# A decoder layer on one core: prompt attention's value product by key-value group, on high and low parts

## The chip, the core and the metric

The kernel runs on one core of a Trainium2 chip. The core has a matrix engine (PE, its weight loads listed as PEld), a vector engine (DVE), a scalar engine (ACT), GpSimd (POOL) and a sync engine (SP) that issues most DMAs. Each engine takes its instructions strictly in the order in which the program lists them; semaphores tie the engines together. SBUF holds the working tiles, PSUM has eight banks of 128x512 fp32 into which PE writes. The metric is the time of one execution on the device in microseconds (us), the median of several runs.

## What is computed

One decoder layer for a prompt of 1024 tokens and for 8 sequences with 4 new tokens each (the sample). Cut to the part around the change, for one chunk of 128 prompt tokens:

```python
def nsa_attend(q, ..., gates):            # 8 query heads, 2 key-value groups, 4 heads per group, head size 64
    p_c = masked_softmax(q . k_cmp);  o_c = p_c @ v_cmp      # compressed blocks: 63 keys
    p_s = masked_softmax(q . k_sel);  o_s = p_s @ v_sel      # selected blocks (all earlier keys for this length)
    p_w = masked_softmax(q . kv_win); o_w = p_w @ v_win      # window of 512 keys
    return g0 * o_c + g1 * o_s + g2 * o_w
```

Beside attention the layer has a state-space part (a scan over 128 steps, a kernel K, a product Y), a GLU on it, an output projection (the mix) and a feed-forward net (FFN). Everything is fp32; sums must keep nearly fp32 accuracy.

## The kernel before, in words

In the order of the span: projections and compression (0 to about 440 us), prompt attention with what is put between its units (about 457 to 950 us), the mix (to about 1085 us), the FFN (to the end).

**Prompt attention** (`phase_attend`) takes the eight chunks of 128 queries in the order 4, 0, 6, 1, 7, 2, 5, 3. Chunk c has, for branch 0 (selected), c+1 key tiles of 128 keys, for branch 1 (window), at most 5, and the compressed branch with 64 keys. A *unit* is a chunk, a branch and four heads. In before, unit `hf` holds heads 2hf, 2hf+1, 4+2hf, 5+2hf, two of each key-value group. `attend_scores` makes a unit's scores and exponentials: fp32r products into a two-bank tile (PSUM tag s), a reduction on DVE (`asm`), an exponential on ACT (`ap`). `attend_values` makes the unit's value product. The scores of the next unit are listed ahead of a unit's values.

**The value product** is made by `pv_tile`, once for each key tile of a unit: PE transposes the four heads' 128x128 probabilities into one PSUM bank (tag t, two banks), ACT or DVE in turn copies the bank to SBUF as fp32 (`pT`), and PE multiplies in plain fp32: two matmuls, one per group, of 64 value columns against 256 query columns, into 64 partitions each of the result bank `O` (tag o, one bank for both units of a branch). This is called a *turn* below. `attend_out` then copies O (128x512) on ACT, PE transposes it, DVE multiplies with the gate over the softmax sum, POOL adds to `att`. The compressed branch does the same with two turns of 64 keys.

**Between the units** stand pieces of other work, by the table PLAN: the sample's second half (A), the state-space kernel (K: products `Kp`, evicted on DVE and ACT to `K`, an addition `dd`, and eight DMAs on SP that spread `K` into `ssm_W`), the outputs Y (from `ssm_W` and the scan's state `ssm_H`), GLU (`gl`), adaLN columns (`ada`), the loading of the output weights (P). They use one PSUM bank of their own (tag f). The list scheduler that builds the program sets the final order on each engine.

**The scan** is 128 steps on DVE, four small SBUF-to-SBUF operations each (lines L1536 to L1539), spread between the other DVE work of chunks 4 and 0.

**The sample's second half** reads its caches through eight buffers `s_raw`; window rows come by SP's DMAs, selected rows by POOL's gathers, two runs of four ahead.

**The mix** (`mix_product`) makes three fp32r matmuls per weight tile from high and low parts of x and of the weights. Its first two row tiles (8 and 7) are listed in the midst of chunks 2, 5 and 3.

Of the kernel before, what the change touches and what calls it, by code (L numbers as in the profile page):

```python
# [89 lines left out]
class Kernel:  # L90
# [235 lines left out]
    def phase_sample(self):  # L326
# [22 lines left out]
        self.sample_begin(sb)  # L349
# [8 lines left out]
        self.compress_end(cp)  # L358
        self.second = self.sample_attend(1, sb)
# [5 lines left out]
        self.XT = "ff"  # L365
# [168 lines left out]
    def c_out(self, b, s, hid):  # L534
# [15 lines left out]
        else:  # L550
            for g in range(2):
                nc.tensor.matmul(p[:64, 64 * g:64 * g + 64], hid[:, g, :64], w2, start=True, stop=True)
            nc.vector.memset(self.vcp, 0.0)
            nc.vector.tensor_scalar(self.vcp[:64], p[:64, :128], 0.5, None, op0=ALU.mult)
# [107 lines left out]
    def sample_attend(self, half, sb):  # L662
# [6 lines left out]
        if half == 0:  # L669
            self.before = sb.tile([128, 30, 30], F32, name="before")  # L670
            o = CONST_AT["before"][0]
            nc.sync.dma_start(self.before.rearrange("p j i -> p (j i)"), A["consts"][:, o:o + 900])
# [51 lines left out]
        runs = [r for r in self.runs if r[0] == half]  # L724
# [7 lines left out]
        for k, run in enumerate(runs):  # L732
# [25 lines left out]
            self.sample_load(sb)  # L758
# [21 lines left out]
    def sample_begin(self, sb):  # L780

        self.runs = [(half, br, j) for half in range(2) for br, j in ((2, 0), (1, 0), (1, 1), (1, 2), (1, 3))]
        self.todo = list(self.runs)
        for _ in range(2):
            self.sample_load(sb)

    def sample_load(self, sb):
        if not self.todo:
            return
        half, br, j = run = self.todo.pop(0)  # L790
        raws = []
        for b in range(4 * half, 4 * half + 4):
            raw = sb.tile([128, 4, 256], F32, tag="s_raw", name=f"s_raw{br}{b}_{j}", bufs=8)
# [4 lines left out]
            raws.append(raw)  # L798
        self.raws[run] = raws
# [207 lines left out]
    def phase_attend(self):  # L1007
# [5 lines left out]
        self.psum("psc", s=2, t=2, o=1, f=1)  # L1013
# [5 lines left out]
        for n, c in enumerate(self.ORDER):  # L1019
# [8 lines left out]
            for br in range(2):  # L1028
                for hf in range(2):
                    ahead.append((c, br, hf, st, self.attend_scores(c, br, hf, st, pa)))  # L1030
# [12 lines left out]
    def between(self, c):  # L1043
# [4 lines left out]
        def part(i):  # L1048
            tags, self.tags = self.tags, "ff"
# [86 lines left out]
    def attend_setup(self, pc, pa):  # L1136
# [6 lines left out]
        self.mk = mk  # L1143
# [81 lines left out]
    def attend_values(self, c, br, hf, st, Ps, pc):  # L1225
# [3 lines left out]
        if hf == 0:  # L1229
            st["O"] = self.ps("o", f"aso{c}{br}")  # L1230
# [675 lines left out]
```

## Time and profile before

| | us |
|---|---|
| median of 3 runs (lowest, highest) | 1826.65 (1823.66, 1833.36) |
| the profiled execution, its own time | 1828.84 |
| its span in the profile | 1827.1 |
| PE busy | 1709.1 (94%) |
| DVE / ACT / POOL busy | 972.2 / 618.9 / 427.1 |
| mean granted PE clock of the execution | 0.979 |

The page gives busy time over the whole span; the share of a stage is read from the table by stretches. "Idle before" a row names what released it. A row with x4 covers four instructions; from the start of one row to the start of the next is what they cost on a busy engine, since the shown length of a matmul holds its pipeline too.

### The profile page before, as it was taken

How to read it: one execution, taken by the hardware profiler on the slowest of the kernel's cores; microseconds unless marked ns; L12 is line 12 of the kernel's file. 1: busy time of each engine (PE TensorE's matmuls, PEld its weight loads, DVE VectorE, ACT ScalarE, POOL GpSimd, SP SyncE). 2: the span in 40 equal slices, each digit the busy share in tenths (PEclk: the TensorE clock that was granted, in tenths of full speed). 3: DMA queues.
4: the chain of work that ended last, by engine and by line, in shares of the span. 5: the costliest groups of instructions: out<-in, count | busy, mean ns of one | idle time of the engine just before them, and what ended most of it. 6: DMA issues, size and time to landing. Idle time of an engine off the chain costs nothing.

```text
span 1827.1 us, 29355 instructions
## 1 busy us (share of the span) xinstructions
PE 1709.1 (94%) x11546; PEld 1439.4 (79%) x11546; DVE 972.2 (53%) x2330; ACT 618.9 (34%) x1247; POOL 427.1 (23%) x817
## 2 busy tenths in 40 slices
PE   6998999899796899999989989999999999999997
PEld 3898988788564665655657888998998999999996
DVE  4867647588988466566535443323333333333346
ACT  4523146455453355565433341111111111211210
POOL 2344545232015313341122210110110110110150
PEclk9999999899898999999999999999999999999999
DMA  8333243645231345413114221101201201201113
GB/s 297 105 86 106 70 152 119 219 157 193 65 112 63 71 161 195 152 61 104 55 60 138 92 93 58 58 24 50 67 24 47 70 24 47 70 24 47 53 47 141
DMA packets 132699, 172.43 MB, mean 94 GB/s; under 512 B 17176, under 2 KB 92312, under 8 KB 132304
## 3 DMA queue, kind: packets, MB, share of 16 engines
q1 hardware_dynamic: 123024, 136.62, 23.4%
q0 software_dynamic: 9408, 33.89, 5.8%
q8 instruction: 91, 1.49, 0.3%
q14 instruction: 48, 0.39, 0.1%
q10 hardware_dynamic: 128, 0.04, 0.0%
HBM read 143.88 MB, written 25.46 MB: 93 GB/s over the span
## 4 chain that ended last, share of the span: by engine, by line
PE 61%; DVE 6%; DMA 4%; ACT 2%; issue 1%; POOL 1%; SPq 1%; DVEq 0%; ACTq 0%; POOLq 0%
PE gu L1810 19%; PE dn L1853 13%; PE g L1810 5%; PE u L1810 4%; PE aso L1283 3%; PE as L1205 1%; PE as L1206 1%; SPq L1596 1%; PE acs L1258 1%; PE mx8M L1728 1%; PE mx2M L1728 1%; PE mx5M L1728 1%; PE mx0M L1728 1%; PE mx1M L1728 1%; PE mx4M L1728 1%
## 5 line engine op out<-in xcount | busy, mean ns | idle before, releaser
L1810 PE MATMUL gu<-h2h,wh 128*128 128x352 f32 x704 | 227.8, 324 | 5.0 <-ACT h2h L870 5.0
L1810 PE MATMUL gu<-h2h,wl 128*128 128x352 f32 x704 | 227.3, 323 | 0.0
L1810 PE MATMUL gu<-h2l,wh 128*128 128x352 f32 x704 | 226.8, 322 | 0.0
L1859 DVE TENSOR_TENSOR acc<-acc,dn 128x512 f32<-128x512 f32 x144 | 98.9, 687 | 229.9 <-PE dn L1853 229.9
L1818 POOL TENSOR_TENSOR al<-fa,ah 128x352 fp32r<-128x352 f32 (+1 forms) x66 | 69.6, 1054 | 414.8 <-ACT ah L1817 408.8
L1813 ACT ACTIVATE fa<-gu 128x352 f32<-128x352 f32 x44 | 20.4, 465 | 412.1 <-PE gu L1810 412.1
L1853 PE MATMUL dn<-dh,ah 128*128 128x512 f32 x352 | 140.3, 399 | 5.6 <-DVE fin L1862 5.2
L1810 PEld LDWEIGHTS gu<-h2h,wh 128*128 128x128 f32 x704 | 132.5, 188 | 7.9 <-ACT h2h L870 5.3
L1853 PE MATMUL dn<-dl,ah 128*128 128x512 f32 x352 | 138.7, 394 | 0.0
L1853 PE MATMUL dn<-dh,al 128*128 128x512 f32 x352 | 138.3, 393 | 0.0
L1810 PEld LDWEIGHTS gu<-h2l,wh 128*128 128x128 f32 x704 | 133.0, 189 | 3.8
L1810 PEld LDWEIGHTS gu<-h2h,wl 128*128 128x128 f32 x704 | 132.7, 188 | 3.1
L1816 DVE TENSOR_TENSOR fa<-fa,gu 128x352 f32<-128x352 f32 x44 | 22.9, 521 | 143.0 <-ACT fa L1813 143.0
L409 ACT CAST wh<-wr 128x1024 fp32r<-128x1024 f32 x44 | 46.0, 1048 | 151.8 <-PE g L1810 77.0
L1205 PE MATMUL as<-kst,aqA 128*128 128x320 f32 (+4 forms) x192 | 76.7, 403 | 16.2 <-ACT ap L1222 9.3
L1853 PEld LDWEIGHTS dn<-dh,ah 128*128 128x128 f32 x352 | 66.1, 188 | 24.5 <-ACT wh L409 7.5
L410 DVE TENSOR_TENSOR wl<-wr,wh 128x1024 fp32r<-128x1024 f32 x44 | 58.8, 1339 | 49.3 <-ACT wh L409 49.3
L1853 PEld LDWEIGHTS dn<-dl,ah 128*128 128x128 f32 x352 | 66.1, 188 | 15.6
L1853 PEld LDWEIGHTS dn<-dh,al 128*128 128x128 f32 x352 | 66.3, 188 | 8.1
L1222 ACT ACTIVATE ap<-as,asm 128x640 f32<-128x640 f32 (+3 forms) x64 | 55.8, 873 | 46.6 <-DVE asm L1221 31.3
L1221 DVE TENSOR_REDUCE asm<-as 128x1 f32<-128x640 f32 (+3 forms) x64 | 58.5, 918 | 20.7 <-PE as L1209 19.8
L1206 PE MATMUL as<-kst,aqB 128*128 128x320 f32 (+4 forms) x192 | 65.1, 344 | 4.7 <-ACT aqB L1168 4.7
(2137 smaller groups left out, 4667.9 us busy)
## 6 DMA issues: line engine op xcount, KB each, us to landing
wada<-in_w_ada SPq DMA_DIRECT2D x24, 1024.0 KB
wr<-in_w_ffn_gate SPq DMA_DIRECT2D x22, 512.0 KB
wr<-in_w_ffn_up SPq DMA_DIRECT2D x22, 512.0 KB
wd<-in_w_ffn_down SPq DMA_DIRECT2D x22, 512.0 KB
bx<-in_x_prompt SPq DMA_DIRECT2D x8, 512.0 KB
s_raw<-in_cache_kv_win SPq DMA_DIRECT2D x8, 512.0 KB
wor<-in_w_out SPq DMA_DIRECT2D x16, 256.0 KB
ex<-x_d SPq DMA_DIRECT2D x8, 512.0 KB
```

The lines of the kernel that those rows point to most:

```text
L409: self.nc.scalar.copy(hi, raw)
L410: self.nc.vector.tensor_tensor(lo, raw, hi.bitcast(F32), op=ALU.subtract)
L1205: nc.tensor.matmul(Sv, qA[:, h, :], kk, start=True, stop=False)
L1206: nc.tensor.matmul(Sv, qB[:, h, :], kk, start=False, stop=not mt)
L1221: nc.vector.tensor_reduce(mx[:, :1], Sv, axis=ax, op=ALU.max, negate=True)
L1222: nc.scalar.activation(Pv, Sv, AF.Exp, bias=mx[:, :1], accum_out=l[:, h:h + 1])
L1283: nc.tensor.matmul(O[64 * g:64 * g + 64, 256 * hf:256 * hf + 256], V[:n, 64 * g:64 * g + 64], pT[:, 256 * g:256 * g + 256], start=first, s ...
L1728: nc.tensor.matmul(M[:P, :], X[k][b], w[:, k, c], start=m == 0, stop=m == 23)
L1810: nc.tensor.matmul(gu[i], w[:, k, :], h[:, k, 352 * n:352 * n + 352], start=m == 0, stop=m == 23)
L1818: nc.gpsimd.tensor_tensor(al[:, cols], a[:, :w], ah[:, cols].bitcast(F32), op=ALU.subtract)
L1853: nc.tensor.matmul(p, a[:, sl], w[:, c], start=m == 0, stop=m == 5)
L1859: nc.vector.tensor_tensor(o, o, p, op=ALU.add)
```

## The change

- **Units by group.** Unit `grp` holds the heads 4grp to 4grp+3, which share one key-value group. The number of units, LOOK, ORDER and PLAN stay.
- **The turn.** `pv_turn` has the same four transposes. ACT then copies the bank as the high part `pTh` (fp32r) and DVE subtracts it from the bank to give the low part `pTl` (fp32r): both engines in each turn, one after the other, where before it was one of them in turn. Two fp32r matmuls of 128 columns of V against 512 query columns follow, two turns late. The V tile `avv` holds the high part in the 64 columns that belong to the group and the low part in the other 64; it is made on POOL for each unit by `value_parts` (a cast and a subtraction of 128 x 64 per key tile).
- **The join.** O now has the high part's product in 64 partitions and the low part's in the other 64. `pv_join` copies one on ACT and adds the other on DVE (64x512 each), once per unit; `attend_out` starts from its result. There are 6 joins per chunk (48 in all) in place of 3 copies (24).
- **The compressed branch**: one turn for all eight heads, then eight fp32r matmuls of 256 columns, with V in a zero-padded tile `vch` made once.
- **PSUM**: s=2, t=2, o=2. The work between the units has no bank f any more and shares the two banks o with O.
- **Pools**: the tiles of the mix (`g1`, X parts) lie in a new pool `wx`, opened after the attention's pools are closed.
- **The sample's second half** opens its own pool after the first half's is closed: six buffers `s_raw` instead of eight, nothing loaded ahead from the first half, and the constant `before` is loaded again.

The diff, cut to its core:

```diff
-        self.psum("psc", s=2, t=2, o=1, f=1)
+        self.psum("psc", s=2, t=2, o=2)
...
-        for h in (2 * hf, 2 * hf + 1, 4 + 2 * hf, 5 + 2 * hf):
+        for h in range(4 * grp, 4 * grp + 4):
...
-        for t in range(nk):
-            self.pv_tile([P[:, t * 128:t * 128 + 128] for P in Ps], self.vst[:, k0 + t, br, :], O, hf, pc, f"as{c}{br}{t}", t == 0, t == nk - 1)
-        st["between"](2 * br + hf)
-        if hf == 0:
+        vv = pc.tile([128, 8, 2, 64], F32R, tag="avv", name=f"avv{c}{br}{grp}")[:, :nk]
+        self.value_parts(vv.rearrange("p t a d -> p a t d"), self.vst[:, k0:k0 + nk, br, 64 * grp:64 * grp + 64], grp)
+        late = []
+        for t in range(nk + 2):
+            if t < nk:
+                late.append(self.pv_turn([P[:, t * 128:t * 128 + 128] for P in Ps], pc, f"as{c}{br}{grp}{t}"))
+            if t > 1:
+                V = vv[:, t - 2].rearrange("p a d -> p (a d)")
+                for n, x in enumerate(late.pop(0)):
+                    nc.tensor.matmul(O, V, x, start=t == 2 and n == 0, stop=t == nk + 1 and n == 1)
+        if grp == 0:
+            st["ot"] = pc.tile([128, 512], F32, tag="aot", name=f"as{c}{br}ot")
+        self.pv_join(st["ot"], O, grp)
+        st["between"](2 * br + grp)
+        if grp == 0:
...
+    def value_parts(self, out, v, grp):
+
+        nc = self.nc
+        hi, lo = out[:, grp], out[:, 1 - grp]
+        nc.gpsimd.tensor_copy(hi, v)
+        nc.gpsimd.tensor_tensor(lo, v, hi.bitcast(F32), op=ALU.subtract)
...
-        self.flip = not self.flip
-        (nc.scalar.copy if self.flip else nc.vector.tensor_copy)(pT, p)
-        for g in range(2):
-            nc.tensor.matmul(O[64 * g:64 * g + 64, 256 * hf:256 * hf + 256], V[:n, 64 * g:64 * g + 64], pT[:, 256 * g:256 * g + 256],
-                             start=first, stop=last)
...
+        h, lo = (pc.tile([128, 512], F32R, tag="apT" + x, name=f"{name}pT{x}", bufs=3) for x in "hl")
+        nc.scalar.copy(h, p)
+        nc.vector.tensor_tensor(lo, p, h.bitcast(F32), op=ALU.subtract)
+        return h, lo
...
+        own, other = slice(64 * grp, 64 * grp + 64), slice(64 - 64 * grp, 128 - 64 * grp)
+        nc.scalar.copy(ot[own], O[other])
+        nc.vector.tensor_tensor(ot[own], ot[own], O[own], op=ALU.add)
...
         self.close("pa", "pc", "kv", "par")
+        self.wx = self.open("wx", bufs=2)
...
+        self.close("sb")
+        sb = self.open("sb")
+        self.sample_begin(sb, 1, 6)
```

The scheduler's order moves with it. PE, ahead of the state-space output `Y` of the first quarter, in before: the end of seven turns of chunk 6 (`as600pt` to `as606pt`).

```order
L1586 MATMUL Kp_8041<-Ct_7726,ssm_par 16x128 x4
L1283 MATMUL aso_8335<-as604pT_8372,vst 64x256 x2
L1279 MATMUL as606pt_8391<-ident,ap_7940 128x128
L1279 MATMUL as606pt_8391<-ident,ap_7950 128x128
L1279 MATMUL as606pt_8391<-ident,ap_7960 128x128
L1279 MATMUL as606pt_8391<-ident,ap_7970 128x128
L1608 MATMUL Y_8067<-ssm_W_7711,ssm_UT_7709 128x128 x8
```

The same place after: chunk 0's joins and its compressed transposes; no turn of chunk 6 stands there, the first comes behind the second `Y`.

```order
L1622 MATMUL Kp_8142<-Ct_7804,ssm_par 16x128 x4
L1248 MATMUL aso_8227<-as0110pTh,avv_8228 128x512
L1248 MATMUL aso_8227<-as0110pTl,avv_8228 128x512
L1329 MATMUL as01otp<-ident,as01ot 128x128 x4
L1311 MATMUL ac0pt<-ident,pcb_6830 128x128 x4
L1622 MATMUL Kp_8245<-Ct_7813,ssm_par 16x128 x4
L1622 MATMUL Kp_8258<-Ct_7813,ssm_par 16x128 x4
L1644 MATMUL Y_8168<-ssm_W_7789,ssm_UT_7787 128x128 x8
L1649 MATMUL Y_8168<-Ct_7793,ssm_H 128x128 x2
L1649 MATMUL Y_8168<-Ct_7794,ssm_H 128x128 x2
```

DVE, at the last step of the scan (`ssm_H` of step 127), in before: the first evictions of `K` stand beside it.

```order
L1538 TENSOR_TENSOR scan0_127_4992<-scan0_127_4992,scan1_127_4993 128x32
L1589 COPY K0_7988<-Kp00_7989 16x128
L1281 COPY ac0pT1_8255<-ac0pt1_8256 64x512
L1539 TENSOR_TENSOR ssm_H_3445<-ssm_H_3445,scan0_127_4992 128x32
L1589 COPY K0_7988<-Kp00_7989 16x128
L1589 COPY K0_7988<-Kp01_8002 16x128
```

After: two evictions of chunk 6's queries, reductions of chunk 6's scores (`asm600`, `asm601`, `asm602`) and chunk 0's last two low parts stand around and behind the last step, and the first `K0` comes after them.

```order
L1574 TENSOR_TENSOR scan0_127_4992<-scan0_127_4992,scan1_127_4993 128x32
L1575 TENSOR_TENSOR ssm_H_3445<-ssm_H_3445,scan0_127_4992 128x32
L1175 CAST aqB6_8010<-aqt61_8012 64x512
L1164 TENSOR_TENSOR aqhl1_9058<-aq1_8027,aqhl1_9058 128x8x64
L1229 TENSOR_REDUCE asm600_8032<-as600_8031 128x1
L1229 TENSOR_REDUCE asm601_8042<-as601_8041 128x1
L1314 TENSOR_TENSOR as0100pTl_8081<-as0100pt_8075,as0100pTh_8080 128x512
L1314 TENSOR_TENSOR as0110pTl_8237<-as0110pt_8231,as0110pTh_8236 128x512
L1229 TENSOR_REDUCE asm602_8052<-as602_8051 128x1
L1625 COPY K0_8089<-Kp00_8090 16x128
```

PE, the mix of row tile 8 (`mx8M`): in before it stands between turns of chunk 5.

```order
L1279 MATMUL as502pt_10869<-ident,ap_10703 128x128
L1279 MATMUL as502pt_10869<-ident,ap_10713 128x128
L1728 MATMUL mx8M_11688<-woh,mx8Xh_11674 32x512
L1728 MATMUL mx8M_11688<-woh,mx8Xl_11675 32x512
L1728 MATMUL mx8M_11688<-wol,mx8Xh_11674 32x512
```

After: it stands behind the last compressed product (`aco` of chunk 3), at the end of attention. The same holds for row tile 7.

```order
L1270 MATMUL aco_12081<-ac3pTl,vch 128x2x128
L1270 MATMUL aco_12081<-ac3pTh,vch 128x2x128
L1270 MATMUL aco_12081<-ac3pTl,vch 128x2x128
L1329 MATMUL ac3otp<-ident,ac3ot 128x128 x4
L1752 MATMUL mx8xt_12136<-ident,mx8xc 128x32 x4
L1764 MATMUL mx8M_12155<-woh,mx8Xh_12141 32x512
```

## Rows read from the trace of the kernel before

**Rows 1.** The page, part 1: busy us (share of the span) and instructions, by engine.
```profile
PE 1709.1 (94%) x11546; PEld 1439.4 (79%) x11546; DVE 972.2 (53%) x2330; ACT 618.9 (34%) x1247; POOL 427.1 (23%) x817
```
**Rows 2.** Stretches: length, busy us of PE, PEld, DVE, ACT, POOL; clock, DMA share, GB/s.
```profile
440.00:600.00 160.00, 131.32 (x1123) 93.05 (x1115) 140.57 (x486) 72.44 (x173) 48.38 (x58) 0.90 0.29 97
600.00:840.00 240.00, 220.33 (x1749) 145.02 (x1748) 147.24 (x248) 138.62 (x310) 69.44 (x221) 0.98 0.42 134
840.00:960.00 120.00, 111.88 (x697) 71.99 (x697) 57.34 (x92) 50.09 (x117) 22.55 (x81) 1.00 0.17 59
960.00:1085.00 125.00, 116.06 (x613) 102.07 (x612) 64.14 (x96) 48.89 (x94) 26.72 (x111) 0.97 0.37 116
```
**Rows 3.** Timeline of PE, chunk 3's turns: start, length, engine, line, operation.
```profile
936.74 0.66 PE L1279 MATMUL as313pt<-ident,ap 128*128 128x128 f32 x4
937.33 0.65 PE L1283 MATMUL aso<-as312pT,vst 128*64 128x256 f32 x4
937.91 0.66 PE L1279 MATMUL as310pt<-ident,ap 128*128 128x128 f32 x4
```
**Rows 4.** Timeline of PE in the mix: four transposes between fp32r matmuls.
```profile
969.02 0.60 PE L1716 MATMUL mx0xt<-ident,mx0xc 128*128 128x128 f32 x4
969.37 0.47 PE L1728 MATMUL mx5M<-woh,mx5Xh 128*128 128x512 f32 x1
969.68 0.39 PE L1728 MATMUL mx5M<-woh,mx5Xl 128*128 128x512 f32 x1
969.91 0.39 PE L1728 MATMUL mx5M<-wol,mx5Xh 128*128 128x512 f32 x1
```
**Rows 5.** Timeline of PE, ACT and DVE: a GLU tile transposed, then its two parts.
```profile
730.13 0.66 PE L1110 MATMUL gl1st<-ident,gl1s 128*128 128x128 f32 x4 [1.11 <-DVE gl0t L1121]
730.83 0.59 ACT L1113 CAST gl1h<-gl1st 128x512 fp32r<-128x512 f32 x1
731.45 0.69 DVE L1114 TENSOR_TENSOR gl1l<-gl1st,gl1h 128x512 fp32r<-128x512 f32 x1
```
**Rows 6.** Timeline of PE at the end of attention: chunk 3's compressed branch.
```profile
945.79 0.63 PE L1279 MATMUL ac3pt<-ident,pcb 128*64 128x128 f32 x4 [0.45 <-DVE as31ot L1300]
946.35 0.65 PE L1283 MATMUL aco<-ac3pT,vcp 64*64 64x256 f32 x4
```
**Rows 7.** Groups of DVE and PE by line, 600 to 960 and 840 to 960 us: count | busy, mean ns.
```profile
L1221 DVE TENSOR_REDUCE asm<-as 128x1 f32<-128x640 f32 (+3 forms) x44 | 41.2, 940 | 19.0 <-PE as L1209 18.8
L1728 PE MATMUL mx7M<-woh,mx7Xh 128*128 128x512 f32 x16 | 6.5, 404 | 0.0
```
**Rows 8.** Timeline of DVE and POOL while POOL works for the kernel K.
```profile
563.75 1.31 DVE L1372 TENSOR_TENSOR ssm_hs<-ssm_ts,ssm_ts 128x128 f32<-128x128 f32 x1
571.02 0.28 DVE L1375 TENSOR_TENSOR ssm_hs<-ssm_ts,ssm_ts 128x128 f32<-128x128 f32 x1
563.69 1.23 POOL L1370 TENSOR_TENSOR Ctt<-ssm_par 128x576 f32<-128x576 f32 x1
```
**Rows 9.** Timeline of DVE, SP and PE from the scan's last step to the second Y.
```profile
586.25 0.24 DVE L1539 TENSOR_TENSOR ssm_H<-ssm_H,scan 128x32 f32<-128x32 f32 x1
590.68 1.19 DVE L1594 TENSOR_TENSOR K<-K,dd 16x128 f32<-16x128 f32 x1
591.93 5.20 SPq L1596 DMA_DIRECT2D ssm_W<-K  x8
598.67 1.95 PE L1608 MATMUL Y<-ssm_W,ssm_UT 128*128 128x128 f32 x16
601.69 5.07 SPq L1596 DMA_DIRECT2D ssm_W<-K  x8
608.16 2.83 PE L1608 MATMUL Y<-ssm_W,ssm_UT 128*128 128x128 f32 x16 [3.32 <-DMA ssm_W<-K]
```

**Rows 10.** Of 440 to 560 us: the page's DMA line, and POOL's first gather for a third run.
```profile
s_raw<-in_cache_kv_slc,idx POOLq DMA_INDIRECT x16, 6.4
494.81 0.94 POOL L404 DMA_INDIRECT s_raw<-in_cache_kv_slc,idx  x1 [45.05 <-PE s120o L850]
```

More of the change, by code (lines that the diff above doesn't have):

```diff
@@ L668, in sample_attend @@
         acc = sb.tile([128, 64], F32, tag="s_acc", name=f"s_acc{half}", bufs=2)
[L669 to L672, printed above, removed]
+        self.before = sb.tile([128, 30, 30], F32, name=f"before{half}")
+        o = CONST_AT["before"][0]
+        nc.sync.dma_start(self.before.rearrange("p j i -> p (j i)"), A["consts"][:, o:o + 900])
         p = self.ps(self.XT[0], f"sc{half}")
@@ L723, in sample_attend @@
                                 nm[:, None, :].to_broadcast([128, 2, 32]), op=ALU.add)
-        runs = [r for r in self.runs if r[0] == half]
+        runs = self.runs
         M, L, R = {}, {}, {}
@@ L778, in sample_attend, with sample_begin, sample_load @@
         nc.sync.dma_start(self.attn_s[128 * half:128 * half + 128], acc)
[L780 to L793, printed above, removed]
+    def sample_begin(self, sb, half, held):
+        self.runs = [(half, br, j) for br, j in ((2, 0), (1, 0), (1, 1), (1, 2), (1, 3))]
+        self.todo = [(run, b) for run in self.runs for b in range(4 * half, 4 * half + 4)]
+        self.held = held
+        self.sample_load(sb, held)
+    def sample_load(self, sb, n):
+        for _ in range(min(n, len(self.todo))):
+            run, b = self.todo.pop(0)
+            _, br, j = run
+            raw = sb.tile([128, 4, 256], F32, tag="s_raw", name=f"s_raw{br}{b}_{j}", bufs=self.held)
             if br == 2:
@@ L1028, in phase_attend @@
             for br in range(2):
-                for hf in range(2):
-                    ahead.append((c, br, hf, st, self.attend_scores(c, br, hf, st, pa)))
+                for grp in range(2):
+                    ahead.append((c, br, grp, st, self.attend_scores(c, br, grp, st, pa)))
                     while len(ahead) > self.LOOK[n]:
@@ L1143, in attend_setup @@
         self.mk = mk
+        self.vch = pc.tile([128, 2, 2, 2, 64], F32R, name="vch", bufs=1)
+        nc.gpsimd.memset(self.vch.bitcast(F32), 0.0)
+        for e in range(2):
+            rows = slice(64 * e, 64 * e + 64)
+            for grp in range(2):
+                self.value_parts(self.vch[rows, e, grp], self.vcp[rows, 64 * grp:64 * grp + 64], grp)
         pcb = [pc.tile([128, 8, 64], F32, name=f"pcb{i}", bufs=1) for i in range(2)]
@@ L1723, in mix_product @@
             c = slice(512 * hf, 512 * hf + 512)
-            M = self.ps("of"[hf] if last else "f", f"{nm}M{hf}")
+            M = self.ps("o", f"{nm}M{hf}")
             m = 0
```

72 lines of the change are left out of this document (38 added, 34 removed).

## The prediction

> **What bounds the kernel now.** I read the page's busy times first, then the table by stretches, then the timelines of single turns. PE is busy 94% of the span [rows 1], but that is an average. Between 440 and 600 us, where chunks 4 and 0 run beside the scan, DVE is busy 140.6 of 160 us and PE 131.3 [rows 2]: there DVE sets the pace, and PE loses 28.7 us. Between 600 and 960 us, the other six chunks, PE is busy 332 of 360 us, DVE 205 and ACT 189 [rows 2]: there PE sets the pace. In the mix PE is busy 116 of 125 us, and the FFN behind it does not change. So the same edit is worth different things before and after 600 us. The sum is made against the profiled execution, 1828.84 us. That is 2.2 us above the median of 1826.65, and I take the 2.2 off at the end. About 0.5% (9 us) is what a measurement of this kernel can tell from no change.
>
> **The turn on PE.** Turns that stand alone cost 937.91 - 936.74 = 1.17 us each [rows 3]: 0.59 for the transposes, 0.58 for the fp32 products. After, four transposes and two fp32r matmuls of 512 columns. The mix has exactly that sequence: transposes 969.37 - 969.02 = 0.35 us, the first matmul behind them 0.31, the next 0.23 [rows 4], together 0.89. That is 0.28 us less per turn. Chunk c has c+1 key tiles in branch 0 and at most 5 in branch 1, so 36 + 30 = 66 tiles, two units each: 132 turns, 24 of them in chunks 4 and 0, 108 in the six later chunks.
>
> **What the turn must now wait for.** Before, one engine evicts a bank; now ACT copies and DVE subtracts, one behind the other. The GLU tile already does this: from the first transpose at 730.13 to the end of the low part at 731.45 + 0.69 it is 2.01 us [rows 5]. With two banks t that is 1.0 us per turn when nothing stands between turns. Where scores or GLU work stands between them, PE fills the wait and the 0.89 is reached. I take half of the 108 turns at 1.0 and half at 0.89: a gain of 0.22 on average, 108 x 0.22 = **-24 us**. The ends: all at 0.89 give 108 x 0.28 = -30. If a reduction of 0.94 us [rows 7] stands ahead of every fourth low part in DVE's queue, the pace is 1.0 + 0.24 = 1.24, and 108 turns lose 0.07 each: +7. By sums of work DVE would not be full: it gets a low part of 0.69 instead of every second eviction, 54 x 0.69 = 37 us, and 36 joins of up to 0.69 = 25, so 205 + 62 = 267 of 360. So I stay near the first end.
>
> The row shows an engine chain of 2.01 us against 0.89 us of PE work [rows 5, 4]. The Trainium skill, page "TensorEngine Tiling (Array Packing)", section "PSUM Bottleneck", speaks against the change here: once the matrix engine is made faster, emptying PSUM may become the bottleneck, and it advises to spread that over both engines; this change puts both in series on every bank. Where that holds for every turn, the later chunks gain nothing; that is the third rival below.
>
> **Compressed branch.** A piece costs 946.35 - 945.79 = 0.56 us [rows 6], four pieces 2.2. After: 0.35 plus eight matmuls of half the columns, 8 x 0.115 = 0.92, so 1.3, but behind the 2.01 us chain and two joins. In six later chunks the ends are -5 and +1; I take **-2**.
>
> **Mix and tail.** The mix of row tiles 8 and 7, 96 matmuls in six groups of 16 [rows 7] at 0.23 = 22 us, leaves chunks 2, 5 and 3 and comes behind attention. PE's sum is the same. It covered waits in 840 to 960 us, where PE still idles 8 us [rows 2]; without it more turns stand alone. I take **+3** (0 to +6). The last unit now ends with the 2.01 us chain and a join of a copy and an addition (0.59 + 0.69 as in rows 5, in place of one copy): **+2** (+1 to +3). Later chunks together: -24 - 2 + 3 + 2 = **-21** (ends -34 and +17).
>
> **Chunks 4 and 0, until the second Y.** PE saves 24 x 0.28 and some in two compressed branches, but DVE is the bound, so I count nothing. Four terms are added.
> - Scan. By the order, ahead of the scan's last step stand 23 low parts instead of 14 evictions and 8 joins, and 4 reductions and 4 smaller operations fewer: 17 x 0.69 - 4 x 0.94 - 4 x 0.69 = **+5** (0, if DVE's 19 idle us take it, to +6).
> - POOL makes `avv` in the scan. By 1.23 us for 576 elements [rows 8] a chunk-4 unit (320 elements, two operations) costs 1.4 us, a chunk-0 unit 0.3, all eight 6.8. A DVE operation on SBUF data took 1.31 instead of 0.28 beside such a POOL operation [rows 8]. If every us of POOL held DVE, 6.8; I take **+2**, since low parts and reductions read PSUM and can stand there as well.
> - K and W. From the scan's last step (586.25) it took 5.7 us to have K (590.68 + 1.19), then 5.2 us of DMAs on SP, and Y came at 598.67 [rows 9]. After, four reductions, two low parts and two query evictions stand behind the scan and ahead of K's addition, instead of two smaller evictions: 4 x 0.94 + 2 x 0.69 + 2 x 0.69 - 2 x 0.69 = 5.1, **+5** (0 to +7).
> - Turns. Seven turns of chunk 6 stood ahead of or around the first two Y, while SP spread K; now they come behind: 7 x 0.89 = 6.2 us of PE work. The second Y waited 3.3 us anyway [rows 9] and later quarters can hide some; **+2** (0 to +6).
>
> Sum **+14**, ends +2 and +25 with the next paragraph.
>
> The POOL term has a rule beside it. The row shows a stretch of 1.0 us [rows 8]. The Trainium skill, page "SBUF — State Buffer", section "SBUF: two separate sides", says that DVE with two SBUF inputs and GpSimd take one shared port pair as an exclusive lock for a whole instruction. The trace agrees in size; by it the term would be up to 6.8 us instead of 2.
>
> **The sample's second half.** With six buffers only two of a later run's four gathers are out ahead; the others are issued on POOL when a buffer comes free, as the one at 494.81 behind `s120o` [rows 10], and land 6.4 us later. PE takes them in order, with the next run's first two sequences and turns ahead of them. Four runs could wait 0 to 1 us each: 0 in my sum, +4 at the end. Where the cover is gone, up to 6 us a run.
>
> **Sum.** 1828.84 + 14 - 21 = 1821.8, less 2.2: **1820 us** (rounded up), with 1811 to 1829 as this case's own range.
>
> **The rivals.**
> - *PE's saving comes through.* All 108 turns at 0.89 with DVE hidden, -30 - 5 + 0 + 1, and chunks 4 and 0 at +5: 1828.84 - 29 - 2.2 = 1798. For it: 28 us of PE idle in 360, so PE is the bound [rows 2]. Against it: 2.01 us of chain on two banks [rows 5].
> - *No cheaper matmul.* The change saves little because a fp32r matmul between transposes costs 0.31 each time and transposes 0.59: 1.21, no less than 1.17; the order alternates one product and four transposes in many places. The later part is then about 0 to -8, early +8: 1828.84 + 4 - 2.2 = 1831. Against it: 0.35 for transposes in rows 4.
> - *DVE's queue takes over (slower).* One mechanism: a low part stands behind reductions or scan steps, the bank t stays full, and PE, which goes in order, waits. It decides from a pace of 1.17 us per turn, that is from 0.17 us of mean wait on top of the chain. Then the later chunks give 0 - 2 + 3 + 2 = +3, and the early ones +14 or more: 1828.84 + 17 - 2.2 = 1843. For it: DVE at 88% in the early stretch and seven turns moved behind Y; against it: 267 of 360 us later.
>
> **How the numbers follow.** Forecast 0.42, PE's saving 0.22, no cheaper matmul 0.14, DVE's queue 0.22. Faster by over 0.5% means below 1817.5: 0.22 of the second and two fifths of the forecast, 0.38. Slower means above 1835.8: the last case and a little of the third, 0.25. Between: 0.37. The range takes in the centres of the outer cases, 1797 to 1844; what is left out is the halves of these two cases beyond, about 0.2.
>
> **What would show it.** Right: in chunks 6 to 3 turns alone start every 1.0 us, PE's idle time before transposes is released by DVE's low part, the scan ends near 593, the second Y starts near 620. PE-bound rival: turns at 0.89 and 600 to 960 nearly full. No cheaper matmul: products of 0.3 each and transposes of 0.5 or more in turns alone, without idle rows between them. DVE rival: the same releaser as in the forecast with over 0.2 us per turn, and DVE over 85% busy between 600 and 900. The forecast is wrong if the early part costs nothing (scan's end at 586), or if PE waits for gathers by more than 4 us.

## The result, and the profile after

The changed kernel takes 1888.6 us (median; 1886.2 to 1890.7) against 1828.4 for the kernel before on the same chip: a ratio of 1.0344, 95% interval 1.0321 to 1.0367. It is **60 to 63 us slower**: 60 by the two medians, 63 by the ratio; 62 is used below. The forecast was 1820 us with a range of 1797 to 1844, so the forecast and the range were both wrong. The profiled execution of after took 1886.2 us, its span is 1884.4 us, its mean granted clock 0.960 instead of 0.979.

The page, part 1, of after (it answers to [rows 1]):

```profile
PE 1726.6 (92%) x11254; PEld 1479.7 (79%) x11254; DVE 1056.4 (56%) x2443; ACT 669.8 (36%) x1337; POOL 461.3 (24%) x890
```

The change lists fewer PE instructions, 11254 against 11546, and yet PE is busy 17 us longer. The table by stretches (columns as in [rows 2]: length, busy us of PE, PEld, DVE, ACT, POOL; clock, DMA share, GB/s):

```profile
440.00:600.00 160.00, 117.64 (x908) 88.58 (x906) 146.80 (x473) 75.22 (x176) 49.51 (x69) 0.85 0.28 92
600.00:840.00 240.00, 211.67 (x1543) 153.09 (x1543) 161.63 (x267) 138.55 (x311) 80.55 (x230) 0.93 0.36 113
840.00:960.00 120.00, 95.19 (x498) 69.36 (x498) 90.09 (x132) 77.49 (x159) 33.61 (x85) 0.90 0.18 59
960.00:1085.00 125.00, 116.58 (x577) 90.28 (x575) 61.41 (x97) 44.87 (x90) 26.41 (x118) 0.96 0.37 113
```

Between 600 and 960 us, where the gain was to be, PE is busy 307 us where it was 332, and the clock column reads 0.93 and 0.90 where it read 0.98 and 1.00 [rows 2]. PE has less to do there, waits more, and does the rest more slowly. No other engine is near full: DVE is busy 252 of 360 us.

Where the 62 us stand, by the start of the same row in both timelines (us; in before, the mix of row tiles 8 and 7 lies inside attention, 24 us; after, behind it, so the last row is the one to compare):

| start of | before | after | difference |
|---|---|---|---|
| second Y | 608.2 | 616.4 | +8.2 |
| chunk 6's last transposes (`ac6otp`) | 686.3 | 709.6 | +23.3 |
| chunk 2's last transposes (`ac2otp`) | 842.4 | 880.9 | +38.4 |
| first product of mix row tile 6 (all attention is done, tiles 8 and 7 too) | 950.5 | 1009.4 | +58.9 |

About 23 us are lost up to the end of chunk 6, 36 more from there to the mix.

**The turn is as forecast.** Timeline of PE and, below, of ACT and DVE, after, chunk 3 (start, length, engine, line, operation, wait and what released it):

```profile
961.84 0.65 PE L1311 MATMUL as3102pt<-ident,ap 128*128 128x128 f32 x4 [0.16 <-DVE as3100pTl L1314]
962.25 0.47 PE L1248 MATMUL aso<-as3100pTl,avv 128*128 128x512 f32 x1
962.56 0.39 PE L1248 MATMUL aso<-as3101pTh,avv 128*128 128x512 f32 x1
962.84 0.66 PE L1311 MATMUL as3103pt<-ident,ap 128*128 128x128 f32 x4
```
```profile
962.53 0.59 ACT L1313 CAST as3102pTh<-as3102pt 128x512 fp32r<-128x512 f32 x1 [0.47 <-PE as3102pt L1311]
```
```profile
963.15 0.69 DVE L1314 TENSOR_TENSOR as3102pTl<-as3102pt,as3102pTh 128x512 fp32r<-128x512 f32 x1 [0.36 <-ACT as3102pTh L1313]
```

From transposes to transposes 962.84 - 961.84 = 1.00 us, the price of two banks and a chain of 963.15 + 0.69 - 961.84 = 2.00 us. The wait before the transposes is released by DVE's low part. All that as the prediction had it, for a turn whose two engines are free. Over the 108 turns that are made from 600 us on the chain takes 2.87 us on average: the high part starts 0.53 us after its transposes, held up by other work of ACT, most of it exponentials, and the low part 0.25 us after the high part, held up by other work of DVE.

**What it did not have** is this. Timeline of PE, after, chunk 2 to chunk 5:

```profile
874.81 0.53 PE L1270 MATMUL aco<-ac2pTl,vch 128*128 128x256 f32 x1 [1.81 <-DVE ac2pTl L1314]
...
880.85 0.66 PE L1329 MATMUL ac2otp<-ident,ac2ot 128*128 128x128 f32 x4 [3.02 <-DVE ac2ot L1322]
881.34 0.69 PE L1311 MATMUL as5000pt<-ident,ap 128*128 128x128 f32 x4
883.49 0.76 PE L1248 MATMUL aso<-as5000pTh,avv 128*128 128x512 f32 x1 [1.46 <-ACT as5000pTh L1313]
```
```profile
887.86 1.11 PE L1311 MATMUL as5003pt<-ident,ap 128*128 128x128 f32 x4
888.62 0.78 PE L1248 MATMUL aso<-as5001pTl,avv 128*128 128x512 f32 x1
889.20 0.63 PE L1248 MATMUL aso<-as5002pTh,avv 128*128 128x512 f32 x1
889.62 1.05 PE L1311 MATMUL as5004pt<-ident,ap 128*128 128x128 f32 x4
```

And the same stretch by 5 us, columns as above:

```profile
880.00:885.00 5.00, 2.69 (x14) 2.22 (x15) 4.17 (x7) 2.32 (x4) 1.69 (x1) 0.67 0.58 165
885.00:890.00 5.00, 4.25 (x15) 3.00 (x14) 3.94 (x6) 4.48 (x10) 2.48 (x11) 0.50 0.45 151
890.00:895.00 5.00, 4.88 (x31) 4.17 (x29) 3.18 (x8) 4.33 (x9) 1.99 (x5) 0.80 0.65 209
```

At 874.81, 880.85 and 883.49 PE stands for 1.8, 3.0 and 1.5 us, for a low part, a join and a high part. ACT's timeline beside it shows why the high part was late: it stood behind the copy of a tile of the output weights, for which ACT had waited until its DMA landed.

```profile
882.15 0.72 ACT L1070 ACTIVATE woh<-wor,vecs 128x512 fp32r<-128x512 f32 x1 [1.37 <-DMA wor<-in_w_out]
882.78 0.56 ACT L1313 CAST as5000pTh<-as5000pt 128x512 fp32r<-128x512 f32 x1
```

Behind these gaps the granted clock is 0.50, the lower of the two levels (1.2 GHz), and the turn from 887.86 on costs 889.62 - 887.86 = 1.76 us instead of 1.00. So such a wait is paid twice.

PE's waits between 440 and 1000 us, summed over its timeline by what PE waited to do, each wait once: 58.6 us before, 101.0 after. The transposes of a result behind its join (`otp`) take 23.5 of them in 15 places, where before took 4.0 in 6; value products with their transposes 23.1 (14.1), the sample 10.1 (2.1), scores and their queries 24.1 (21.3). Two of the expectations below have 25.0 in 18 places and 5.6: they also count three waits (two in before) in which other instructions waited for such a result, and one wait of before twice.

### The profile page after: what moved, and what is told of

It reads as the page before. It is cut to its first block, busy times and chain, and to the rows that moved or that the text cites. A ratio compares the mean times of both kernels' runs of the same rounds, so it can differ in the third digit from the quotient of the medians.

```text
span 1884.4 us, 29143 instructions
## 1 busy us (share of the span) xinstructions
PE 1726.6 (92%) x11254; PEld 1479.7 (79%) x11254; DVE 1056.4 (56%) x2443; ACT 669.8 (36%) x1337; POOL 461.3 (24%) x890
## 4 chain that ended last, share of the span: by engine, by line
PE 73%; DVE 12%; DMA 6%; ACT 5%; issue 2%; POOL 1%; SPq 1%; DVEq 0%; ACTq 0%; POOLq 0%
PE gu L1846 18%; PE dn L1889 13%; PE g L1846 4%; PE u L1846 4%; PE cp L519 4%; PE aso L1248 2%; DMA s_raw<-in_cache_kv_slc,idx 1%; PE q0p L937 1%; PE kv1p L937 1%; PE q1p L937 1%; PE u1p L937 1%; PE ct L497 1%; PE as L1213 1%; PE kv0p L937 1%; PE as L1214 1%
## 5 line engine op out<-in xcount | busy, mean ns | idle before, releaser
L1213 PE MATMUL as<-kst,aqA 128*128 128x320 f32 (+4 forms) x192 | 75.1, 397 | 13.6 <-ACT ap L1230 7.6
```

Of the source, the lines that this page charges most:

```text
L1213: nc.tensor.matmul(Sv, qA[:, h, :], kk, start=True, stop=False)
```

## The experiments

Two theories for the later chunks. **Joins**: PE, in order, waits at the transposes behind each join. **Chain**: ACT and DVE in series on each bank hold up the turns. Beside them, **clock**: the gaps halve the clock, which multiplies either. Rivals: the lost cover of the mix and of bank f, and in the early part the sample's six buffers. Ratios are to the kernel before on the same chip, with 95% intervals; after itself is 1.0344.

**1 to 3. One part of the change alone, in before.** The mix's pools opened behind attention:

```diff
+        self.wx = self.open("wx", bufs=2)
-            self.g1 = wo.tile([128, 1024], F32, tag="g1", name=f"g1_{tt}", bufs=1)
+            self.g1 = wx.tile([128, 1024], F32, tag="g1", name=f"g1_{tt}", bufs=1)
```

> The kernel before with one part of the change alone: the mix tiles (g1, X parts, xn) lie in a pool that is opened behind attention, so the mix of row tiles 8 and 7 comes behind attention. Theory A (the turn's chain of ACT and DVE on two banks, with the PE clock that falls in the gaps, costs the time): PE's sum is the same and before has only 8 us of idle time there, 1827 to 1834. Theory B (the lost filler costs the time: the moved mix and the shared banks): the 24 us of mix come on top, 1845 to 1855. Theory C (the early stretch with the sample's buffers and the scan): no change, 1825 to 1831.

1.0013 (0.9992 to 1.0035). Inconclusive: `mx8M` still stands inside attention, at 845.7 us, since the pool found room of its own. The two shared result banks, without bank f:

```diff
-        self.psum("psc", s=2, t=2, o=1, f=1)
+        self.psum("psc", s=2, t=2, o=2)
...
-            M = self.ps("of"[hf] if last else "f", f"{nm}M{hf}")
+            M = self.ps("o", f"{nm}M{hf}")
```

> The kernel before with one part of the change alone: two result banks o that the work between the units shares, in place of one o and one f. The mix then shares them too. Theory A: 1825 to 1835. Theory B: fillers are tied to the units by the turn of the banks, and the mix of row tiles 8 and 7 leaves attention; 1845 to 1860. Theory C: no change.

1.0008 (0.9982 to 1.0035). Here the mix does move: timeline of PE of this kernel, the end of attention:

```profile
930.51 0.66 PE L1293 MATMUL ac3otp<-ident,ac3ot 128*128 128x128 f32 x4 [0.69 <-ACT ac3ot L1290]
931.88 0.81 PE L1728 MATMUL mx8M<-woh,mx8Xh 128*32 128x512 f32 x2 [0.35 <-ACT mx8Xh L1718]
```

So neither the mix behind attention nor the sharing of the banks costs anything in before. The sample's six buffers:

```diff
-        self.sample_begin(sb)
+        self.sample_begin(sb, 0, 8)
+        self.close("sb")
+        sb = self.open("sb")
+        self.sample_begin(sb, 1, 6)
```

> The kernel before with one part of the change alone: the sample's second half with a pool of its own, six buffers and no loads ahead. Theory C: PE waits for gathers and for window rows, 5 to 15 us slower, 1832 to 1843. Theories A and B: 1825 to 1830.

1.0057 (1.0037 to 1.0077): 10 us. PE, in the timeline of this kernel, waits for the gathers of the third and fourth sequence of each run:

```profile
523.70 0.66 PE L830 MATMUL s161kt<-ident,s_raw 128*128 128x128 f32 x4 [2.61 <-DMA s_raw<-in_cache_kv_slc,idx]
526.82 1.09 PE L830 MATMUL s171kt<-ident,s_raw 128*128 128x128 f32 x4 [2.47 <-DMA s_raw<-in_cache_kv_slc,idx]
```

Everything else of that edit kept, with eight buffers:

```diff
-        self.sample_begin(sb, 1, 6)
+        self.sample_begin(sb, 1, 8)
```

> The kernel before with the sample's second half in a pool of its own, but eight buffers: nothing is loaded ahead from the first half, and two runs are ahead later. If the six buffers cost the 10 us of the sample's change (a gather is issued behind the product that frees its buffer): 1827 to 1833. If the new pool and the missing loads ahead cost them: 1838 to 1845.

1.0001 (0.9983 to 1.002). The six buffers alone cost the 10 us; the separate pool costs nothing.

**4 and 5. The chain, in after.** First without the low part (one eviction, by ACT or DVE in turn, and one product instead of two):

```diff
-        nc.scalar.copy(h, p)
-        nc.vector.tensor_tensor(lo, p, h.bitcast(F32), op=ALU.subtract)
-        return h, lo
+        self.flip = not self.flip
+        (nc.scalar.copy if self.flip else nc.vector.tensor_copy)(h, p)
+        return (h,)
```

> The changed kernel without the low part of the probabilities (this part of the product is left out): one bank is evicted by ACT or DVE in turn, one fp32r matmul per key tile. Banks, pools, joins and sample stay as changed. PE has 132 matmuls of 0.23 less (30 us). Theory A: the chain falls from 2.0 to about 1.1 us per bank, the clock stays up, 1820 to 1840. Theory B or C: only what PE saves where it is the bound, 1865 to 1885.

1.0119 (1.0076 to 1.0162), still slower than before, although PE has one of two products less. Then the same with the high part multiplied twice, so that PE's work stays:

```diff
-        return (h,)
+        return h, h
```

> The changed kernel with the high part multiplied twice in place of the low part (the low part of the probabilities is left out): PE has the same matmuls as changed, but a bank is evicted once, by ACT or DVE in turn, as before, and DVE has 66 operations less. Theory of the chain: the 41 us of the run without a low part come mostly from the chain and the clock, 1850 to 1865. Theory that PE's work counts: 30 of the 41 us were PE's, so 1875 to 1885.

1.0209 (1.0191 to 1.0227): the chain is worth 1.0344 - 1.0209 = 0.0135, 25 us, with the DVE and ACT work that goes with it; this run does not part the two engines in series from the work that each has in its queue. The other 37 are elsewhere.

**6 to 8. Banks and cover, in after.** Three banks t and one o:

```diff
-        self.psum("psc", s=2, t=2, o=2)
+        self.psum("psc", s=2, t=3, o=1)
```

> The changed kernel with three banks for transposes and one result bank (the work between the units uses the transposes' banks). Theory of the chain (2.0 us of ACT and DVE on two banks pace a turn alone at 1.0): turns alone come at 0.89, later chunks 6 to 20 us faster, 1868 to 1882. Theory of the unit's ends (joins, compressed branch and exponentials make PE wait): turns alone at 0.89 as well, but a unit's first product waits for the join before it; 0 to 15 us slower, 1888 to 1905.

1.0546 (1.0513 to 1.058). With three banks turns alone do start every 0.9 us, not every 1.00; timeline of PE of this kernel, chunk 3:

```profile
955.51 0.60 PE L1311 MATMUL as3010pt<-ident,ap 128*128 128x128 f32 x4
955.87 0.48 PE L1248 MATMUL aso<-as3002pTh,avv 128*128 128x512 f32 x1
956.18 0.39 PE L1248 MATMUL aso<-as3002pTl,avv 128*128 128x512 f32 x1
956.41 0.60 PE L1311 MATMUL as3011pt<-ident,ap 128*128 128x128 f32 x4
```

For the time the run is inconclusive: attention ends 6 us later (`ac3otp` 982.95 against 977.01), and the mix, which has only one bank o, takes 43 us longer from its first product to its last. The old banks back, and then the mix's tiles opened early as well, so that it stands inside attention again (in chunk 2):

```diff
-        self.psum("psc", s=2, t=2, o=2)
+        self.psum("psc", s=2, t=2, o=1, f=1)
```
```diff
+        for tt in self.MIX:
+            self.mix_product(tt)
...
-            self.g1 = wx.tile([128, 1024], F32, tag="g1", name=f"g1_{tt}", bufs=1)
+            self.g1 = self.par.tile([128, 1712], F32, tag="ssm_par", name=f"g1_{tt}")[:, :1024]
```

> The changed kernel with the banks of before: one result bank o, one bank f for the work between the units and for the first two row tiles of the mix (whose tiles still lie in the late pool). Theory of the unit's ends: a unit's first product waits for the join before it, 0 to 10 us slower, 1888 to 1900. If shared banks tie the fillers to the units: 10 to 20 us faster, 1868 to 1880.

> As the run with the banks of before, and the tiles g1 and X of the mix in pools that are open during attention, so that the mix of row tiles 8 and 7 (24 us of PE) stands in chunk 2 again. If PE's waits in the later chunks (43 us idle) are there because nothing fills them: 15 to 30 us faster than the run before it, near 1865. If the waits come from work in order that a filler only pushes back: within 5 us of it.

1.0368 (1.0334 to 1.0403) and 1.0356 (1.0317 to 1.0395). Putting the cover back gains nothing clear of noise; the lost cover isn't the cause.

**9 and 10. The clock, in after.** PE multiplies something that nobody reads, three products ahead of a join's transposes and two ahead of a unit's first value product, 136 in all, 31 us of PE time at full clock:

```diff
+            if t == 2:
+                self.fill(O, 2)
...
+    def fill(self, p, n):
+        k = self.kst[:, 0, 0]
+        for _ in range(n):
+            self.nc.tensor.matmul(p, k[:, :128], k[:, :512], start=True, stop=True, skip_group_check=True)
...
+        self.fill(p, 3)
```

> The changed kernel with 136 more fp32r matmuls of 512 columns (31 us of PE) that only keep PE busy: three into the transposes' bank while PE waits for a join, two into the result bank while it waits for a unit's first high part; what they write is overwritten. Theory of the clock (PE's gaps lower the granted clock, and turns at half clock cost 1.7 in place of 1.0 us): the clock between 660 and 980 rises from 0.92 to 0.97 or more, and the time falls by 5 to 20 us although PE has more work, 1870 to 1884. If the low clock only accompanies the waits: 5 to 30 us slower, 1894 to 1920.

1.0247 (1.0214 to 1.0279). The second time without chunks 4 and 0, where DVE sets the pace; 102 products, 23 us:

> As the run with 136 matmuls that only keep PE busy, but without them in chunks 4 and 0, where DVE sets the pace (102 of them stay, 23 us of PE). Theory of the clock: 1865 to 1878, and after 660 us the clock stays at 0.97 or more. If the earlier gain came from the early chunks: 1884 or more.

1.0247 (1.022 to 1.0275): 18 us **faster** than after with 23 us **more** PE work. The two stretches, after first, then the second of these kernels:

```profile
660.00:840.00 180.00, 159.61 (x993) 110.39 (x993) 127.97 (x204) 114.16 (x257) 58.40 (x193) 0.94 0.39 132
...
840.00:960.00 120.00, 95.19 (x498) 69.36 (x498) 90.09 (x132) 77.49 (x159) 33.61 (x85) 0.90 0.18 59
```
```profile
660.00:840.00 180.00, 166.36 (x1073) 118.14 (x1071) 126.37 (x206) 116.38 (x261) 54.78 (x177) 0.98 0.39 130
840.00:960.00 120.00, 104.20 (x590) 77.22 (x590) 94.47 (x142) 81.39 (x167) 36.68 (x102) 0.99 0.19 62
```

The clock goes from 0.94 and 0.90 to 0.98 and 0.99. Busy time times the missing share of the clock, summed over stretches of 5 us from 660 to 980: 3.1 us before, 20.2 after, 4.7 here. The difference of 15.5 is nearly the whole gain. (Between 440 and 660 us the same sum is 12.6 before, 21.7 after and 21.2 here.) The Trainium skill, page "TensorE: Matmul & The Clock Gate", section "A second HAM failure mode: psum-queue depth-cycling", tells of a kernel that cycles through PSUM banks and whose short idle times between groups of matmuls make the clock go to and fro; the trace agrees, with a granted clock of 0.50 to 0.80 behind waits of 1.5 to 3.0 us.

**11 and 12. The joins as work, in after.** PE adds the two halves itself, by a product with two identities on top of each other; ACT copies whole banks, DVE's additions are gone:

```diff
-        nc.scalar.copy(ot[own], O[other])
-        nc.vector.tensor_tensor(ot[own], ot[own], O[own], op=ALU.add)
+        self.nc.scalar.copy(ot, O)
...
+                nc.tensor.matmul(p[:, r * 128 + 64 * grp:r * 128 + 64 * grp + 64], o[:, r * 128:r * 128 + 128], self.both, start=True, stop=True)
```

> The changed kernel with the join on PE: ACT copies the whole result bank once per unit, and the transposes become products with a 128x64 matrix of two identities, which add the two halves; DVE's 48 additions are gone. Theory of the joins (PE waits 25.0 us for joins and their transposes in place of 5.6 before, 18 waits): most of the 19 us goes and the clock rises, 1860 to 1875. Theory of the chain per turn alone: the joins lie off the path that counts, 1884 to 1892.

1.0304 (1.0276 to 1.0332). It does shorten the waits at `otp` (2.4 us left after 690), but there are twice as many products as transposes before, and each is recorded as two instructions; PE's rows of chunk 6's result, after first, then this kernel:

```profile
709.62 0.66 PE L1329 MATMUL ac6otp<-ident,ac6ot 128*128 128x128 f32 x4 [1.44 <-DVE ac6ot L1322]
```
```profile
715.82 1.09 PE L1331 MATMUL ac6otp<-vcp,ac60ot 128*128 128x64 f32 x8
717.19 1.00 PE L1331 MATMUL ac6otp<-vcp,ac61ot 128*128 128x64 f32 x8
```

From `ac6otp` to `ac3otp` these rows take 30.8 us (128 products) instead of 8.9 (64 transposes). The gain is eaten by 22 us of PE work, so this run says little of the joins' waits. The same without the low part:

> The join on PE and no low part of the probabilities (this part of the product is left out): one eviction per turn, one copy per unit, DVE no busier than before, PE with 60 us of matmuls less than before. If PE's saving is lost only to the chain and the joins: faster than before by what PE saves in the later chunks, 1790 to 1815. If the saving turns into waits for exponentials and a lower clock: 1825 to 1845.

1.007 (1.0048 to 1.0091): both kinds of waits are shortened and one product in two is gone, and it is still not faster than before. That is the second of the two ranges.

**13 and 14. The joins as waits, in after.** All work is kept; only the place changes. A unit's result transposes are listed behind the next unit's first two turns, the compressed ones (and the chunk's norm) behind the next chunk's first two:

```diff
+            if t == min(2, nk) and self.later:
+                self.later.pop()()
...
-        self.attend_out(st["ot"], l, att, pc, f"as{c}{br}", br == 0)
         if br == 0:
+            self.later.append(lambda: self.attend_out(st["ot"], l, att, pc, f"as{c}{br}", True))
             return
```

> The changed kernel with all its work, but a unit's last transposes are listed behind the next unit's first two turns, and the compressed branch's too, so PE does not stand still for the join. Theory of the joins (25 us of PE's waits, and the clock that falls in them): 1860 to 1875, and PE's wait for joins falls below 8 us. If other waits take their place: 1880 to 1890.

1.0155 (1.0137 to 1.0174): 34 us. Timeline of PE of this kernel, the end of attention:

```profile
947.43 0.66 PE L1339 MATMUL as31otp<-ident,as31ot 128*128 128x128 f32 x4
...
950.01 0.66 PE L1339 MATMUL ac3otp<-ident,ac3ot 128*128 128x128 f32 x4 [1.45 <-DVE ac3ot L1332]
```

In after these two stand at 971.40 and 977.01 and wait 1.39 and 1.47 us; here, at the end of attention, only the very last, which has no next unit to hide behind, still waits for its join. In all of attention these transposes still wait in 5 places for 10.7 us (23.5 in 15), 5.8 of them in one place where the last releaser is not a join but ACT's eviction of queries. From 660 to 840 and from 840 to 960 us the clock is 0.95 and 0.94 instead of 0.94 and 0.90; by the sum used above 12.1 us are lost to it instead of 20.2, so about 8 of the 34 us are the clock's. Both remedies together, the edits of a single eviction with the high part twice and of the late transposes:

> Both edits: no chain (the low part is left out, PE's matmuls kept) and deferred transposes. If chain and joins are two causes that add: the two gains add, 1825 to 1845. If they share the same lost time (one gap takes the other's place): no more than 8 us below the better of the two.

1.0033 (1.0016 to 1.0049). The gains add: 25 + 34 = 59 us singly, 57 together. What the clock takes between 660 and 980 us is 18.7 us with the chain alone out and 5.6 with both out.

**15. The same remedy in before.** Late listing of the result transposes, nothing else (`rest` holds them and what follows them):

```diff
+            while t == min(1, nk - 1) and self.later:
+                self.later.pop(0)()
...
+        def rest():
             p = self.ps_t(name + "otp")
...
+        return rest
```

> Before, with each selected branch's result transposes (as..otp) listed behind the next unit's first turns, and chunk's compressed ones (ac..otp) behind the next chunk's; the copy of O stays where it was, so no work is left out. If the joins cost what they do because PE waits in order at those transposes, the same remedy is worth in before only what PE idles there: 5.6 us by its timeline, so ratio 0.997 to 1.000 (1823 to 1828 us). A rival, that the late listing itself frees something else (banks, DVE's queue) and gave the changed kernel its 34 us, would give before over 10 us as well: ratio below 0.994. If it is slower, the late listing costs something of its own and the 34 us are a lower bound.

0.994 (0.9918 to 0.9961): 1815.8 us, **the fastest kernel of this study**, 11 us below before. That is more than before idles at these transposes (4.0 us), so the rival has a part in it. PE's waits between 440 and 1000 us fall from 58.6 to 47.1 us: transposes of results 4.0 to 0.7, compressed products 5.5 to 0.8, scores and their queries 21.3 to 13.6, the mix 5.4 to 0.6 (K and Y give 8 back, the selected and window products 5). Two rows of it, from the end of chunk 3, where before has [rows 6]:

```profile
934.50 0.66 PE L1307 MATMUL as31otp<-ident,as31ot 128*128 128x128 f32 x4
935.08 0.65 PE L1295 MATMUL aco<-ac3pT,vcp 64*64 64x256 f32 x4
```

The transposes now fill the wait of the compressed product, which waits no longer in this chunk. Why the scores wait less too was not taken apart. For the joins of the changed kernel it means that some 11 of the 34 us would have been there to gain before as well.

**The sum.** With the late listing on both sides the change costs 1.0155 - 0.994 = 0.0215, 39 us; so its own joins cost about 62 - 39 = 23 us. With the chain out too, 1.0033 - 0.994 = 0.0093, 17 us are left. Chain 22 (39 - 17) to 25, joins 23, sample 10 (measured alone in before): 55 to 58 of the 62 us. The clock is no term beside these; its loss lies inside them. By the intervals each of these differences is open by 4 to 7 us to either side, so the rest is no more than the runs leave open.

Where the last 17 us stand is seen by the same rows in before with late listing and, second, in the changed kernel with both remedies: the second Y starts at 607.5 and 608.4, `ac6otp` (behind two turns of chunk 1 in both) at 681.9 and 701.2, the first product of mix row tile 6 at 938.3 and 952.8. So 19 us are lost by the end of chunk 6, and from there on the change is 5 us faster (251.6 against 256.4 us; 264.2 in before itself). In a kernel without the low part's chain and with late listing the cheaper turns do show as time, then, behind chunk 6. With the low part made they do not: late listing alone leaves 268.5 us there. Of the 19 us up to chunk 6 the sample's buffers explain some 10; the rest was not taken apart and stays open.

## Why the prediction was wrong, step by step

- **The bound.** "There PE sets the pace" was read from 332 of 360 us busy [rows 2], and that reading was right for before. The step from there to the sum, in which a cheaper turn is worth nearly its difference, failed. In before a turn's eviction was short enough to be hidden in the order as listed; after, what PE waits for is longer.
- **The turn alone, 1.00 us; the product prices.** Right: 1.00 us, half the chain of [rows 5], against 1.17 in [rows 3]; and at full clock 0.36, 0.31 and 0.23 in the medians, as from [rows 4].
- **The later chunks, -21 (ends -34 and +17).** Wrong in sign; measured +36 in the five chunks behind chunk 6 alone. From `ac6otp` to `ac3otp` the turns (transposes and value products) take PE 104.0 us after and 93.3 before, waits of 0.15 us and more not counted. Some 12 of the 104.0 are what the rows at half clock cost beyond their price at full clock; without these it is 92, so almost nothing was gained even there, where 84 turns at 0.89 would have been 75. Shorter waits are still in the 92. Two terms were missing. First, **the joins**: costed as work of DVE ("36 joins of up to 0.69 = 25") and as +2 at the tail. They are a copy and an addition in series, 970.66 + 0.69 - 970.05 = 1.30 us, in 48 places; behind 24 of them, the second of each branch, PE's next instructions are the transposes of the result or are soon followed by them, and in 15 PE stood still there, 1.6 us on average. One of them, timeline of ACT, DVE, PE's loads and PE, after:

```profile
970.05 0.58 ACT L1321 COPY as31ot<-aso 64x512 f32<-64x512 f32 x1 [1.31 <-PE aso L1248]
970.66 0.69 DVE L1322 TENSOR_TENSOR as31ot<-as31ot,aso 64x512 f32<-64x512 f32 x1 [1.20 <-ACT as31ot L1321]
971.40 0.42 PEld L1329 LDWEIGHTS as31otp<-ident,as31ot 128*128 128x128 f32 x4 [1.71 <-DVE as31ot L1322]
971.40 0.66 PE L1329 MATMUL as31otp<-ident,as31ot 128*128 128x128 f32 x4 [1.39 <-DVE as31ot L1322]
```

  The tail's own reasoning (the last unit ends with a chain and a join) was right, and held for the end of every branch, not for the last unit alone. The joins are worth 23 us of the change's own, 34 with what late listing gains anyway. Second, **the clock**: all prices were taken at full clock. Its loss of 20.2 us between 660 and 980, 17 more than before, had no term (it comes with the waits and is contained in what joins and chain cost), and there was a hint of it, the 0.90 of the early stretch in [rows 2].
- **The chain.** "Half of the 108 turns at 1.0 and half at 0.89" became 25 us of loss, measured by taking the chain out. The 2.01 us were read from a tile whose engines were free; the 108 turns took 2.87 on average. ACT's queue was given no term, though ACT makes every high part besides the exponentials: from 600 us on PE waits 10.2 us for high parts and 4.7 for low parts. The rule on PSUM was given as a reason for a third rival of 1843. The Trainium skill, page "TensorEngine Tiling (Array Packing)", section "PSUM Bottleneck", was nearer to the truth than my half and half: emptying the banks held PE up, and no engine had to be full for it.
- **The mix, +3.** Nothing to be seen in before (1.0008); in after, putting it back gained nothing.
- **The scan, +5; K and W, +5.** Right in size. In after the scan ends at 585.8 us, 0.7 earlier than in before, which is the prediction's own sign for an early part that costs nothing; but the attention before it also began 5.7 us earlier (`s013o` 438.7 against 444.4), so it took 5.0 us longer. From the scan's end to the end of K's addition it takes 11.6 us, where [rows 9] give 5.4. Timeline of DVE, SP and PE, after:

```profile
584.58 1.17 DVE L1575 TENSOR_TENSOR ssm_H<-ssm_H,scan 128x32 f32<-128x32 f32 x1
587.11 2.08 DVE L1229 TENSOR_REDUCE asm<-as 128x1 f32<-128x896 f32 x2
...
596.50 0.81 DVE L1630 TENSOR_TENSOR K<-K,dd 16x128 f32<-16x128 f32 x1
...
607.67 5.07 SPq L1632 DMA_DIRECT2D ssm_W<-K  x8
...
615.66 0.67 DVE L1652 COPY y<-Y 128x512 f32<-128x512 f32 x1
616.39 3.49 PEld L1644 LDWEIGHTS Y<-ssm_W,ssm_UT 128*128 128x128 f32 x16 [5.12 <-DVE y L1652]
616.39 3.78 PE L1644 MATMUL Y<-ssm_W,ssm_UT 128*128 128x128 f32 x16 [4.84 <-DVE y L1652]
```

  The second Y starts at 616.4, forecast "near 620". But it isn't late by its DMAs, which have landed by 612.7: it waits for the eviction of the first Y. Up to the second Y the whole early part measures +8.2 us from the span's start and +13.9 from `s013o`, against +14 in the sum. That is in part luck: the sample was put at 0, and its buffers alone, in before, moved the second Y by 8 us, counted from `s013o`; and the seven turns of chunk 6 that moved behind Y were not yet paid by then.
- **POOL and DVE in the scan, +2.** No run tells this one apart. The Trainium skill's rule on the shared port, "SBUF — State Buffer", section "SBUF: two separate sides", can so be neither confirmed nor refuted by the change; the scan took 5.0 us longer, where the terms for it and for POOL add up to 7.
- **The sample, 0 (up to +4).** Wrong in size: 10 us alone. The text had the price ("where the cover is gone, up to 6 us a run") and didn't use it. In after 3.9 us are still to be seen as waits for gathers.
- **The range.** Even all the bad ends together, 1828.8 + 25 + 17 - 2.2 = 1869, would not have reached 1889: what was missing were terms (joins and clock, a chain behind other work, the sample) and not wider ends.
- **The rival that ended slower** had PE waiting in order behind DVE, at more than 1.17 us per turn. The pace was reached: 104.0 us by half of 168 value products is 1.24 us per turn, and a low part stood 0.25 us behind other work of DVE, where the rival asked for 0.17. But DVE was 67 and 75% busy after 600 us, not over 85, and ACT's part in the waits was the larger; they come from series of short operations on two engines, not from a full queue. The rival without a cheaper matmul had the result of its sum in common with the measured turns (92 us at full clock against 93.3) but not its reason: alone, products took 0.31 and 0.23 and transposes 0.36.

## What to carry to other kernels

When an engine that goes in order is fed by a short chain of other engines, price the chain by places, not by the share of busy time: so many places, each with the wait that stands there when nothing is listed between, and look in the order for what is listed next. Work that needs a result should be listed behind the next unit's first independent work; that alone was worth 34 us here after the change and 11 us before it. Price a chain with the other work that stands in its engines' queues, too. Here the gaps of PE had a second price, the lower clock behind them, so a change that saves PE work and opens gaps can end slower.

## What was not expected of the hardware

- The granted clock fell to 0.50 behind waits of PE of 1.5 to 3.0 us in a stretch where PE was busy 2.69 of 5 us (880 to 885), and useless products in these gaps made the kernel 18 us faster.
- A plain fp32 product that multiplies only 64 columns costs nearly twice as much as a transpose of 128: it is recorded as two instructions, 0.22 us together at full clock, where a transpose took 0.12.
